# Sparse-attention layer: compressed scores that stay in PSUM, one reciprocal for two score slots at a longer pipeline distance, and query tiles assembled by DMA

## The chip, the cores and the metric

The kernel runs on one core of a Trainium2 chip. The metric is the device time of one execution in microseconds (us). The core has TensorE (PE; its weight loads are listed apart as PEld), VectorE (DVE), ScalarE (ACT), GpSimd (POOL) and SyncE (SP, which issues most of the DMAs here). L1058 means line 1058 of the kernel before, unless the text says that it is a line of the changed one.

## The reference

One layer of a decoder on x of 1 x 512 x 1024 in float32. After a norm and one input projection, two mixers run side by side: a pooling mixer, and attention with 16 heads of 64 (two groups of keys and values) in three branches: compressed keys, selected blocks, sliding window. With 512 tokens, all blocks are picked and the window covers everything, so the last two branches are plain causal attention on keys of their own. A squared-ReLU MLP follows.

```python
proj = rms_norm(x, norm_mix) @ w_in          # u, q, 3 x (k, v), gates
q  = apply_rope(q);  ks = apply_rope(ks);  kw = apply_rope(kw)
k_cmp = apply_rope(compress(kc)); v_cmp = compress(vc)     # 31 keys
p_c = masked_softmax(q @ k_cmp.T * scale);   o_c = p_c @ v_cmp
p_s = masked_softmax(q @ ks.T * scale);      o_s = p_s @ vs
p_w = masked_softmax(q @ kw.T * scale);      o_w = p_w @ vw
y_nsa = g0 * o_c + g1 * o_s + g2 * o_w
merged = g_a * (pool_mixer(u) @ w_proj_pool) + g_b * (y_nsa @ w_proj_nsa)
x = x + merged @ w_out
x = x + square(relu(rms_norm(x) @ w_ff1)) @ w_ff2
return rms_norm(x, norm_final)
```

## The kernel before

Products are made accurate by splitting each float32 operand into a high part, as float32r, and a low part, the difference; PE then multiplies high by high, high by low and low by high. A high part is a copy on ACT, a low part a subtraction on DVE (sometimes POOL).

There are three stages. The first (until about 170 us) holds the input projections and their preparation. The second is the attention stage (about 182 to 391 us), where the change lies. The third holds the output projections and the MLP.

**Slots.** The attention stage works on 8 pairs of heads with 12 slots each. A slot is one head's block of 128 queries: for the first two query blocks a slot holds both causal branches (two softmax blocks each), for the other two each branch has a slot of its own. So 96 slots hold 128 softmax blocks, and two neighbours are the two heads of a pair on the same queries. Each slot passes through this chain:

- PE computes the scores into a PSUM bank of tag S (`score_pe`, L1013, with Q against high and low keys);
- DVE adds the mask and takes the minimum in one operation (`smax`, L1035), which writes P to SBUF and the minimum into `sm`; scores are kept with their sign turned, so the minimum is the softmax's maximum;
- ACT takes the exponential with the row sum (`expo`, L1045);
- DVE inverts the sum (L1055) and POOL multiplies P by it and by the branch's gate (`weight`, L1058);
- PE transposes P into a bank of tag T (`turn_pe`, L1075), ACT copies the high part (L1086), DVE subtracts the low part (`turn_lo`, L1090);
- PE multiplies by the values into psO (`pv`, L1109). ACT and DVE empty psO (`o_evac`, L1116, L1118).

The loop over slots does the parts of several slots at each turn: scores of i+1, transposes of i − LAG, softmax of i, weights of i − 1, and PV of i − LAG − 2; with LAG 4 and five P buffers. Between them it places matmuls of the remaining projections (L394), which fill PE, and one step of each side generator. The order written here is then rearranged by a scheduler that fixes one list for each engine. PSUM has three banks of tag S, two of T, two of F (projections) and one of O.

**Side generators.** `cmp_scores(p)` handles the compressed keys of one pair, from slot 3 of the pair before: eight matmuls into psC, a bank of tag S (L950); DVE adds the mask (L957), adds the second half of the scores (L958), takes the minimum (L960) and subtracts it (L962), all but the two additions within SBUF tile `cw`; ACT takes the exponential (L965); DVE sums and inverts (L967, L968, L970); POOL weights and splits (L972, L974, L975).

`rope` prepares one pair's queries from a projection's PSUM result: ACT copies them into `rx` (L618), four DMAs on SP write the swapped halves into `rs` (L621), POOL multiplies both by cosine and sine in the attention stage (L626, L629, two of 128x256 each), DVE adds (L634, twice). Then `q_done` makes the tile Q (three buffers): ACT copies the high parts of the two heads (L659, L660) and DVE subtracts the low parts (L662, L664), each 64 partitions by 512; Q holds high and low parts of one head below each other, so that one matmul sums over both. Tiles rx and rs have one buffer each. Three of the eight pairs' queries are prepared in the first stage, five in the attention stage.

SP's queue also carries the weight loads (`raw`, L235) and parts of sums of MLP weights (L265); POOL issues other parts of these sums (L273), and does the low parts of some projection weights (L353).

Of the kernel before, what the change touches and what calls it, by code (L numbers as in the profile page):

```python
# [13 lines left out]
F32 = mybir.dt.float32  # L14
FR = mybir.dt.float32r
AF = mybir.ActivationFunctionType
# [8 lines left out]
DH = 64  # L25
NT = S // 128
S_BANKS, T_BANKS, F_BANKS = 3, 2, 2
LAG, PLAG = 4, 2
P_BUFS, PT_BUFS = 5, 3
CMP_AT = 3  # L30
BIG = 1e30
EPS = 1e-6
# [30 lines left out]
def trunk(ctx: ExitStack, tc: tile.TileContext, A, out):  # L63
# [548 lines left out]
    def rope(ps, scale, done, after=0):  # L612

        assert not scored["rope"]
        scored["rope"] = 1
        xr = ap.tile([128, S], F32, tag="rx", bufs=1, name="rx")
        sw = ap.tile([128, S], F32, tag="rs", bufs=1, name="rs")
        ACT.activation(xr, ps, AF.Copy, scale=scale)  # L618
        for b in range(4):
            a = b ^ 1  # L620
            nc.sync.dma_start(sw[32 * b:32 * b + 32, :], xr[32 * a:32 * a + 32, :])  # L621
        yield
        eng = POOL if mode["pool"] else DVE
        hs = [slice(0, S // 2), slice(S // 2, S)]
        for c in hs:
            eng.tensor_tensor(xr[:, c], xr[:, c], cosT[:, c], op=ALU.mult)  # L626
            yield
        for c in hs:
            eng.tensor_tensor(sw[:, c], sw[:, c], sinT[:, c], op=ALU.mult)  # L629
            yield  # L630
        yield
        for c in hs:
            yield
            DVE.tensor_tensor(xr[:, c], xr[:, c], sw[:, c], op=ALU.add)  # L634
        while scored["pairs"] < after:
            yield
        for _ in done(xr):
            yield
        scored["rope"] = 0

    def k_done(br):
        def done(k):
            for g in range(2):
                r = [slice(64 * h, 64 * h + 64) for h in range(2)]
                src = k[r[g], :].rearrange("p (a b) -> p a b", a=4)
                for h in range(2):
                    ACT.activation(KH[g][r[h], :, br, :], src, AF.Copy)
                yield
                DVE.tensor_tensor(KL[g][r[g], :, br, :], src, KH[g][r[g], :, br, :].bitcast(F32), op=ALU.subtract)
                yield  # L650
                ACT.activation(KL[g][r[1 - g], :, br, :], KL[g][r[g], :, br, :].bitcast(F32), AF.Copy)
        return done
# [1 line left out]
    Q = {}  # L654

    def q_done(p):
        def done(q):
            t = ap.tile([128, 2, S], FR, tag="Q", bufs=3, name="Q")
            ACT.activation(t[0:64, 0, :], q[0:64, :], AF.Copy)  # L659
            ACT.activation(t[64:128, 1, :], q[64:128, :], AF.Copy)  # L660
            yield
            DVE.tensor_tensor(t[64:128, 0, :], q[0:64, :], t[0:64, 0, :].bitcast(F32), op=ALU.subtract)  # L662
            yield
            DVE.tensor_tensor(t[0:64, 1, :], q[64:128, :], t[64:128, 1, :].bitcast(F32), op=ALU.subtract)  # L664
            Q[p] = t
        return done

# [222 lines left out]
    with ExitStack() as c2:  # L890
# [54 lines left out]
        def cmp_scores(p):  # L945
            g = p // 4
            ps = ps2.tile([128, NT, 2, 64], F32, tag="S", bufs=S_BANKS, name="psC")
            for qb in range(NT):
                for h in range(2):
                    PE.matmul(ps[:, qb, h, :], Q[p][:, h, 128 * qb:128 * qb + 128], KC[g], start=True, stop=True,  # L950
                              skip_group_check=True)
            w = p2.tile([128, NT, 2, 64], F32, tag="cw", bufs=1, name="cw")
            s8 = p2.tile([128, 3, 8], F32, tag="c8", bufs=1, name="c8")
            cm = cst[:, C_CM:C_CM + 128].rearrange("p (q n) -> p q n", q=NT)
            wl = w[:, :, :, 0:32]
            wf = w.rearrange("p q h n -> p (q h) n")[:, :, 0:32]
            DVE.tensor_tensor(wl, ps[:, :, :, 0:32], cm[:, :, None, :].to_broadcast([128, NT, 2, 32]), op=ALU.add)  # L957
            DVE.tensor_tensor(wl, ps[:, :, :, 32:64], wl, op=ALU.add)  # L958
            yield
            DVE.tensor_reduce(s8[:, 0, :], wf, axis=AX.X, op=ALU.min)  # L960
            yield
            DVE.tensor_tensor(wf, wf, s8[:, 0, :, None].to_broadcast([128, 8, 32]), op=ALU.subtract)  # L962
# [12 lines left out]
            POOL.tensor_tensor(pL, wl, pH.bitcast(F32), op=ALU.subtract)  # L975
            yield
            yield
            yield
            yield
            pt = ps2.tile([128, S], F32, tag="T", bufs=T_BANKS, name="psT")  # L980
            for qb in range(NT):
                src = PC[:, qb, :, :].rearrange("p e c -> p (e c)")
                PE.transpose(pt[:, 128 * qb:128 * qb + 128].bitcast(FR), src, identR)
            t = p2.tile([128, S], FR, tag="pc", bufs=1, name="pc")
            ACT.activation(t, pt, AF.Copy)
            PTc[p] = t
# [9 lines left out]
                        slots.append((p, 1, br, qb, h))  # L996

        live = {}
        PT = {}
        O = {}  # L1000

# [14 lines left out]
        def blocks(i):  # L1016
            p, half, br, qb, h = slots[i]
            nb = qb + 1
            if half == 0:
                return [(b, 128 * nb * b, nb) for b in range(2)]  # L1020
            return [(br, 0, nb)]

        def smax(i):
            p, half, br, qb, h = slots[i]
            ps = live[i]
            sm = p2.tile([128, 3, 2], F32, tag="sm", bufs=6, name="sm")
            P = p2.tile([128, S], F32, tag="P", bufs=P_BUFS, name="P")
            for e, (b, o, nb) in enumerate(blocks(i)):
                n = 128 * nb
# [10 lines left out]
        def expo(i):  # L1040
            p, half, br, qb, h = slots[i]
            ps, sm, P = live[i]
            for e, (b, o, nb) in enumerate(blocks(i)):
                c = P[:, o:o + 128 * nb]
                last_exp[:] = [ACT.activation(c, c, AF.Exp, bias=sm[:, 0, e:e + 1], scale=-1.0,  # L1045
                                              accum_out=sm[:, 1, e:e + 1])]

        def weight(i):
            p, half, br, qb, h = slots[i]
            ps, sm, P = live[i]  # L1050
            head = 2 * p + h
            bl = blocks(i)
            nb_ = len(bl)
            c = 3 * head + 1 + bl[0][0]
            DVE.reciprocal(sm[:, 2, 0:nb_], sm[:, 1, 0:nb_])  # L1055
            for e, (b, o, nb) in enumerate(bl):
                n = 128 * nb
                r = POOL.tensor_scalar(P[:, o:o + n], P[:, o:o + n], sm[:, 2, e:e + 1],  # L1058
# [73 lines left out]
        for i in range(n + LAG + PLAG):  # L1132
# [15 lines left out]
            if i < n:  # L1148
                smax(i)
                expo(i)  # L1150
            if 0 <= i - 1 < n:
                last = weight(i - 1)
            if i % 4 == 3 and len(begun) > 1:
                add_sum(last)
            if 0 <= t < n:
# [496 lines left out]
```

## Time and profile before

| | us |
|---|---|
| median of 3 runs | 816.5 (815.71 to 817.32) |
| profiled execution | 814.65 |
| its span, first to last instruction | 812.9 |
| PE busy | 788.6 |
| DVE busy | 627.4 |
| ACT busy | 491.6 |
| POOL busy | 207.8 |
| mean granted clock of TensorE | 0.994 |

The profile comes from the one profiled execution. "Busy" is the sum of the times in which an engine worked on at least one instruction. In a timeline a row is: start, duration, engine, line, operation, output<-inputs, shapes, count, and in brackets the idle time ahead of it with the instruction that ended it. In a group of the lines view the columns are: count, busy us, mean ns of one, idle us of the engine just before them and what ended most of it. A view by source line gives the minimum, median and maximum of one instruction's duration in ns, and the first and last start in us. In a windows view each row is a stretch, its length, busy us (and instructions) of each engine, the granted clock, and the DMA engines' share and rate.

### The profile page before, as it was taken

The page shows a single profiled execution, that of the slowest core. Times are in us where ns is not written, and L with a number is a line of the kernel's source. Part 1 is how long each engine was busy: PE and PEld are TensorE (multiplying, and loading weights), DVE is VectorE, ACT ScalarE, POOL GpSimd, SP SyncE. Part 2 cuts the span into 40 slices and gives each one's busy share as a digit, 9 for nine tenths or more (in the row PEclk, how much of TensorE's full clock was granted, in tenths as well). Part 3 has the DMA queues.
Part 4 walks back from the last instruction along what each step waited for, and adds up shares of the span by engine and source line. Part 5 has one row for each costly group of instructions (what it writes and reads, how often), then busy time and mean ns, then how long its engine had stood idle before and what let it go on. Part 6 is the DMA issues. An engine that isn't in the chain of part 4 may idle for free.

```text
span 812.9 us, 14154 instructions
## 1 busy us (share of the span) xinstructions
PE 788.6 (97%) x5163; PEld 710.2 (87%) x5163; DVE 627.4 (77%) x1217; ACT 491.6 (60%) x968; POOL 207.8 (26%) x273
## 2 busy tenths in 40 slices
PE   8999999998899999999999999999999999999996
PEld 7889878886788888888788899999999999999996
DVE  5796744539879898889664579996889688978975
ACT  6576533337777888899434466943773477347833
POOL 4000000028766867665334100111111110000000
PEclk9999999999999999999999999999999999999999
DMA  9554633357446634553964707999998997754522
GB/s 304 143 158 122 164 92 94 102 170 153 67 124 122 144 79 92 104 131 65 328 152 154 202 9 208 311 243 283 250 286 218 285 266 194 222 164 156 181 79 104
DMA packets 128752, 136.65 MB, mean 168 GB/s; under 512 B 5349, under 2 KB 117001, under 8 KB 128522
## 3 DMA queue, kind: packets, MB, share of 16 engines
q1 hardware_dynamic: 107274, 113.98, 43.5%
q0 software_dynamic: 21120, 20.97, 18.1%
q8 instruction: 41, 0.67, 0.3%
q10 hardware_dynamic: 288, 0.79, 0.3%
q14 instruction: 29, 0.24, 0.1%
HBM read 131.01 MB, written 44.04 MB: 215 GB/s over the span
## 4 chain that ended last, share of the span: by engine, by line
PE 73%; DVE 16%; ACT 6%; issue 3%; DMA 1%; POOL 1%; ACTq 0%; DVEq 0%; POOLq 0%
PE psF L394 22%; PE psB L1379 15%; PE psB L394 12%; PE psB L1498 9%; PE psO L1109 3%; PE psT L1075 3%; PE psS L1013 2%; DVE wl L308 2%; PE psV L394 2%; DVE P L1035 2%; DVE PT L1090 1%; PE psF L451 1%; ACT P L1045 1%; DVE w3l L308 1%; PE psC L714 1%
## 5 line engine op out<-in xcount | busy, mean ns | idle before, releaser
L394 PE MATMUL psF<-R,wh 128*128 128x512 f32 x512 | 166.8, 404 | 0.9 <-ACT GB L688 0.6
L306 ACT ACTIVATE wh<-raw 128x1024 fp32r<-128x1024 f32 x70 | 74.0, 1057 | 74.5 <-PE psB L1498 32.6
L351 ACT ACTIVATE wh<-raw 128x512 fp32r<-128x512 f32 (+1 forms) x100 | 60.2, 620 | 82.2 <-PE psF L394 37.4
L394 PEld LDWEIGHTS psF<-R,wh 128*128 128x128 f32 x512 | 92.5, 189 | 18.7 <-ACT GB L688 0.8
L273 POOL DMA_DIRECT2D S<-w_ff x40 | 46.3, 1158 | 233.0 <-DMA S<-w_ff 162.5
L394 PE MATMUL psF<-R,wl 128*128 128x512 f32 x256 | 101.9, 398 | 0.8 <-DVE wl L353 0.8
L1058 POOL TENSOR_SCALAR P<-P,sm,GT 128x128 f32<-128x128 f32 (+3 forms) x128 | 85.7, 702 | 47.9 <-DVE sm L1055 34.1
L308 DVE TENSOR_TENSOR wl<-raw,wh 128x1024 fp32r<-128x1024 f32 x70 | 85.3, 1220 | 16.0 <-ACT wh L306 15.9
L353 DVE TENSOR_TENSOR wl<-raw,wh 128x512 fp32r<-128x512 f32 (+1 forms) x74 | 53.5, 734 | 32.9 <-ACT wh L351 32.5
L1045 ACT ACTIVATE P<-P,sm 128x128 f32<-128x128 f32 (+3 forms) x128 | 71.1, 557 | 12.1 <-DVE sm L1035 10.8
L1035 DVE CUSTOM_DVE_ANT_0 P<-psS,cst 128x128 f32<-128x128 f32 (+3 forms) x128 | 59.6, 483 | 6.2 <-PE psT L1075 4.6
L1379 PE MATMUL psB<-R,wh 128*128 128x256 f32 x352 | 64.1, 282 | 0.0
L353 POOL TENSOR_TENSOR wl<-raw,wh 128x512 fp32r<-128x512 f32 x28 | 39.0, 1398 | 87.6 <-ACT wh L351 85.2
L306 ACT ACTIVATE w3h<-raw 128x1024 fp32r<-128x1024 f32 x35 | 37.0, 1057 | 39.0 <-PE psB L1498 16.5
L1090 DVE TENSOR_TENSOR PT<-psT,PT 128x512 fp32r<-128x512 f32 (+2 forms) x96 | 56.6, 594 | 4.6 <-ACT PT L1086 3.5
L1086 ACT ACTIVATE PT<-psT 128x512 fp32r<-128x512 f32 (+2 forms) x96 | 49.3, 521 | 15.8 <-PE psT L1075 15.1
L394 PEld LDWEIGHTS psF<-R,wl 128*128 128x128 f32 x256 | 48.3, 188 | 11.8 <-DVE wl L353 0.9
L1075 PE MATMUL psT<-ident,P 128*128 128x128 f32 x320 | 51.6, 276 | 6.4 <-POOL P L1058 5.0
L1075 PEld LDWEIGHTS psT<-ident,P 128*128 128x128 f32 x320 | 40.2, 142 | 17.0 <-POOL P L1058 7.8
L308 DVE TENSOR_TENSOR w3l<-raw,w3h 128x1024 fp32r<-128x1024 f32 x35 | 42.7, 1221 | 15.2 <-ACT w3h L306 15.2
L1379 PEld LDWEIGHTS psB<-R,wh 128*128 128x128 f32 x352 | 54.1, 189 | 0.3 <-DVE R L1321 0.2
L1379 PE MATMUL psB<-R,wl 128*128 128x256 f32 x176 | 49.5, 281 | 0.0
(385 smaller groups left out, 2303.6 us busy)
## 6 DMA issues: line engine op xcount, KB each, us to landing
raw<-w_ff SPq DMA_DIRECT2D x55, 512.0 KB, 5.0
S<-w_ff POOLq DMA_DIRECT2D x40, 512.0 KB, 7.5
raw<-S SPq DMA_DIRECT2D x40, 512.0 KB, 5.1
raw<-w_in SPq DMA_DIRECT2D x32, 512.0 KB, 4.0
S<-w_ff SPq DMA_DIRECT2D x30, 512.0 KB, 5.6
S<-S SPq DMA_DIRECT2D x10, 512.0 KB, 6.6
raw<-w_proj_nsa SPq DMA_DIRECT2D x8, 512.0 KB, 4.1
raw<-w_out SPq DMA_DIRECT2D x8, 512.0 KB, 4.4
```

Of the source, the lines that this page charges most:

```text
L306: ACT.activation(h, t, AF.Copy)
L308: DVE.tensor_tensor(l, t, h.bitcast(F32), op=ALU.subtract)
L351: ACT.activation(h[:, sl], t[:, sl], AF.Copy)
L353: eng.tensor_tensor(l[:, sl], t[:, sl], h[:, sl].bitcast(F32), op=ALU.subtract)
L394: PE.matmul(ps, a, b, start=first and j == 0, stop=last and j == n - 1, skip_group_check=True)
L1035: DVE.tensor_tensor_reduce(out=P[:, o:o + n].rearrange("p (a c) -> p a c", c=128), in0=s, in1=m, scale=1.0, scalar=3e38, op0=ALU.add, op1= ...
L1045: last_exp[:] = [ACT.activation(c, c, AF.Exp, bias=sm[:, 0, e:e + 1], scale=-1.0, accum_out=sm[:, 1, e:e + 1])]
L1058: r = POOL.tensor_scalar(P[:, o:o + n], P[:, o:o + n], sm[:, 2, e:e + 1], GT[:, qb, c + e:c + e + 1], op0=ALU.mult, op1=ALU.mult)
L1075: PE.transpose(pt[:, 128 * j:128 * j + 128], P[:, 128 * j:128 * j + 128], ident)
L1090: DVE.tensor_tensor(dL, src, dH.bitcast(F32), op=ALU.subtract)
L1379: PE.matmul(out, w[u][:, k, 128 * f:128 * f + 128], XB[x][v][:, k, :], **kw)
L1498: PE.matmul(out, YB[y][u][:, k, 128 * f:128 * f + 128], w[v][:, k, :], **kw)
```

## The change

Three parts, all in the attention stage's code; the third also touches the three query pairs that the first stage prepares.

1. In `cmp_scores` the second addition writes its sum back into psC. The minimum and the subtraction then read from psC; the subtraction still writes to `cw` in SBUF.
2. The `sm` tiles of two neighbouring slots become one (four buffers of twice the width), and `invert` takes the reciprocal of both slots' sums at once, at the odd slot (line 1059 of the changed kernel). Weights are made for slot i − 2 instead of i − 1, LAG goes from 4 to 5 and P has six buffers.
3. In `q_done` ACT copies the high part of both heads in one operation into rs, DVE subtracts the low part of both in one operation in place in rx, and four DMAs on SP place the four quarters of 64 x 512 into Q.

```diff
-LAG, PLAG = 4, 2
-P_BUFS, PT_BUFS = 5, 3
+LAG, PLAG = 5, 2
+P_BUFS, PT_BUFS = 6, 3
...
-        def done(q):
+        def done(q, other):
             t = ap.tile([128, 2, S], FR, tag="Q", bufs=3, name="Q")
-            ACT.activation(t[0:64, 0, :], q[0:64, :], AF.Copy)
-            ACT.activation(t[64:128, 1, :], q[64:128, :], AF.Copy)
-            yield
-            DVE.tensor_tensor(t[64:128, 0, :], q[0:64, :], t[0:64, 0, :].bitcast(F32), op=ALU.subtract)
-            yield
-            DVE.tensor_tensor(t[0:64, 1, :], q[64:128, :], t[64:128, 1, :].bitcast(F32), op=ALU.subtract)
+            hi, lo = other.bitcast(FR), q.bitcast(FR)
+            ACT.activation(hi, q, AF.Copy)
+            yield
+            DVE.tensor_tensor(lo, q, other, op=ALU.subtract)
+            yield
+            for h in range(2):
+                r, c = slice(64 * h, 64 * h + 64), slice(64 - 64 * h, 128 - 64 * h)
+                nc.sync.dma_start(t[r, h, :].bitcast(F32), other[r, :])
+                nc.sync.dma_start(t[c, h, :].bitcast(F32), q[r, :])
...
             DVE.tensor_tensor(wl, ps[:, :, :, 0:32], cm[:, :, None, :].to_broadcast([128, NT, 2, 32]), op=ALU.add)
-            DVE.tensor_tensor(wl, ps[:, :, :, 32:64], wl, op=ALU.add)
-            yield
-            DVE.tensor_reduce(s8[:, 0, :], wf, axis=AX.X, op=ALU.min)
-            yield
-            DVE.tensor_tensor(wf, wf, s8[:, 0, :, None].to_broadcast([128, 8, 32]), op=ALU.subtract)
+            sc = ps.rearrange("p q h n -> p (q h) n")[:, :, 0:32]
+            DVE.tensor_tensor(ps[:, :, :, 0:32], ps[:, :, :, 32:64], wl, op=ALU.add)
+            yield
+            DVE.tensor_reduce(s8[:, 0, :], sc, axis=AX.X, op=ALU.min)
+            DVE.tensor_tensor(wf, sc, s8[:, 0, :, None].to_broadcast([128, 8, 32]), op=ALU.subtract)
+            yield
...
-            sm = p2.tile([128, 3, 2], F32, tag="sm", bufs=6, name="sm")
+            if h == 0:
+                shared[0] = p2.tile([128, 3, 4], F32, tag="sm", bufs=4, name="sm")
+            b0 = h * len(blocks(i))
+            sm = shared[0][:, :, b0:b0 + len(blocks(i))]
...
+        def invert(i):
+            n = 2 * len(blocks(i))
+            DVE.reciprocal(shared[0][:, 2, 0:n], shared[0][:, 1, 0:n])
+
         def weight(i):
...
-            DVE.reciprocal(sm[:, 2, 0:nb_], sm[:, 1, 0:nb_])
...
-            if 0 <= i - 1 < n:
-                last = weight(i - 1)
+            if i < n and i % 2:
+                invert(i)
+            if 0 <= i - 2 < n:
+                last = weight(i - 2)
```

More of the change, by code (lines that the diff above doesn't have):

```diff
@@ L636, in rope @@
             yield
-        for _ in done(xr):
+        for _ in done(xr, sw):
             yield
@@ L641, in k_done, with done @@
     def k_done(br):
-        def done(k):
+        def done(k, _):
             for g in range(2):
@@ L998, in trunk @@
         live = {}
+        shared = [None]
         PT = {}
@@ L1052, in weight @@
             bl = blocks(i)
-            nb_ = len(bl)
             c = 3 * head + 1 + bl[0][0]
-            DVE.reciprocal(sm[:, 2, 0:nb_], sm[:, 1, 0:nb_])
             for e, (b, o, nb) in enumerate(bl):
```

## The prediction

> **What bounds the kernel now.** I read the page's first part, then the windows by stretch, then the waits of PE, then the timelines of the engines around each hole of PE.
>
> ```profile
> PE 788.6 (97%) x5163; PEld 710.2 (87%) x5163; DVE 627.4 (77%) x1217; ACT 491.6 (60%) x968; POOL 207.8 (26%) x273
> ```
>
> PE is the bound: 788.6 of 812.9 us. The change leaves PE's work as it is (both programs have 5155 matmuls by my count of their instructions, and the same lists from the end of the attention stage on). So it can only win where PE stands still or at a low clock, inside the attention stage.
>
> ```profile
> core 0: us, PE busy (x) PEld busy (x) DVE busy (x) ACT busy (x) POOL busy (x), PEclk, DMA share, GB/s
> 190.00:200.00 10.00, 6.87 (x33) 5.09 (x32) 9.43 (x22) 4.28 (x12) 8.09 (x12) 0.83 0.63 114
> 200.00:215.00 15.00, 14.37 (x102) 12.85 (x100) 13.73 (x50) 14.37 (x41) 10.78 (x17) 1.00 0.57 86
> 215.00:225.00 10.00, 7.44 (x38) 6.28 (x37) 8.61 (x21) 4.91 (x13) 6.67 (x10) 0.83 0.32 51
> 225.00:240.00 15.00, 14.24 (x79) 11.86 (x78) 11.72 (x36) 11.50 (x31) 9.49 (x15) 1.00 0.31 92
> 240.00:380.00 140.00, 137.93 (x895) 121.04 (x895) 124.41 (x411) 118.91 (x320) 97.93 (x134) 1.00 0.51 109
> ```
>
> From 240 to 380 us PE idles 140 − 137.93 = 2.07 us in all, while DVE is idle for 15.6. There a faster DVE buys next to nothing. Two stretches of 10 us hold idle time and a granted clock of 0.83. What PE waited for there:
>
> ```profile
> 192.98 0.44 PE L1075 MATMUL psT<-ident,P 128*128 128x128 f32 x2 [2.16 <-POOL P L1058]
> 193.76 0.44 PE L1075 MATMUL psT<-ident,P 128*128 128x128 f32 x2 [0.34 <-POOL P L1058]
> 195.75 0.87 PE L1075 MATMUL psT<-ident,P 128*128 128x128 f32 x3 [0.62 <-DVE PT L1090]
> 197.07 0.63 PE L1013 MATMUL psS<-KH,Q 128*128 128x512 f32 x1
> 197.50 0.63 PE L1013 MATMUL psS<-KL,Q 128*128 128x512 f32 x1
> 205.22 0.39 PE L1013 MATMUL psS<-KH,Q 128*128 128x512 f32 x1
> 205.45 0.39 PE L1013 MATMUL psS<-KL,Q 128*128 128x512 f32 x1
> 207.03 0.54 PE L983 MATMUL psT<-identR,PC 128*128 128x128 f32 x4 [0.63 <-DVE PT L1090]
> 217.72 0.96 PE L1075 MATMUL psT<-ident,P 128*128 128x128 f32 x4 [2.47 <-POOL P L1058]
> ```
>
> After each long hole the clock is halved for some 5 us: two score matmuls start 0.43 us apart at 197 us and 0.23 apart at 205. So a hole costs itself and about as much again. **First hole**: from 190.82 (192.98 − 2.16) until the spacing is normal again at 198.35, 7.5 us pass, in which PE does work that takes 2.4 to 2.5 at full clock: 5.0 lost (2.16 + 0.34 + 0.62 idle, about 1.9 to clock). **Second hole**: from 215.25 to the first normal spacing at 222.4, 7.2 us for 2.7 of work: 4.5 lost. With 0.63 at 207.03 and 0.76 of idle in 225 to 240, the stage loses 10.9 us before 240 and 2.1 after it.
>
> The Trainium skill's page "TensorE: Matmul & The Clock Gate", Part 1, has the clock fall to half after an idle window of about 3.4 us; by that rule holes of 2.2 and 2.5 us would cost only themselves. The trace does not agree: the two 10 us stretches around them stand at 0.83.
>
> What makes the two holes is seen on DVE and POOL:
>
> ```profile
> 189.22 4.16 DVE L962 TENSOR_TENSOR cw<-cw,c 128x256 f32<-128x256 f32 x1
> 193.31 0.68 DVE L1035 CUSTOM_DVE_ANT_0 P<-psS,cst 128x512 f32<-128x512 f32 x1
> 189.23 1.83 POOL L626 TENSOR_TENSOR rx<-rx,cst 128x256 f32<-128x256 f32 x2
> 190.63 1.78 POOL L629 TENSOR_TENSOR rs<-rs,cst 128x256 f32<-128x256 f32 x2
> 192.02 2.31 POOL L1058 TENSOR_SCALAR P<-P,sm,GT 128x256 f32<-128x256 f32 x3
> 214.47 2.79 DVE L962 TENSOR_TENSOR cw<-cw,c 128x256 f32<-128x256 f32 x1
> 214.34 1.88 POOL L626 TENSOR_TENSOR rx<-rx,cst 128x256 f32<-128x256 f32 x2
> ```
>
> The subtraction of the compressed scores, 0.41 us long when alone, lasts 4.16 and 2.79 us while POOL multiplies the rotary parts, and holds up everything queued on DVE behind it; POOL's rope stands ahead of the weights (L1058) that PE wants.
>
> **The change, part by part.** *Compressed scores kept in PSUM.* Groups of DVE in 180 to 400 us (count, busy us, mean ns, idle before):
>
> ```profile
> L962 DVE TENSOR_TENSOR cw<-cw,c 128x256 f32<-128x256 f32 x7 | 9.5, 1362 | 0.0
> L958 DVE TENSOR_TENSOR cw<-psC,cw 128x256 f32<-128x256 f32 x7 | 2.9, 416 | 0.0
> L960 DVE TENSOR_REDUCE c<-cw 128x8 f32<-128x256 f32 x7 | 2.9, 410 | 0.1
> ```
>
> The second addition already reads one operand from PSUM and takes 0.416, steadily. The subtraction will do the same: 7 × (1.362 − 0.416) = 6.6 us of DVE saved. Writing the sum into PSUM and the minimum out of it have no row; bounds are 0.41 (as now) and 0.68 (L1035's 512-wide PSUM read), and I take 0.41, the row of the same size. Against it: a bank of the three score banks stays held for two operations more.
>
> The Trainium skill's page "SBUF — State Buffer", section "Who interferes with whom", says that a DVE instruction with two SBUF inputs contends with GpSimd instructions that read SBUF, and one with at most one such input does not; it also says that the loser blocks for one whole instruction. The long L962 agrees with the first part, but 4.16 us spans more than four POOL instructions, so the loser lost again and again. By one instruction's blocking the saving would be 7 × 0.75 = 5.3 at most instead of 6.6.
>
> *One reciprocal for two slots.*
>
> ```profile
> L1013 PE MATMUL psS<-KH,Q x96: 274/392/628, 182.4 to 375.6; 128*128 128x512 f32 x48, 128*128 128x384 f32 x32, 128*128 128x256 f32 x16
> L1055 DVE RECIPROCAL sm<-sm 128x1 f32<-128x1 f32 (+1 forms) x96 | 15.0, 158 | 7.7 <-ACT P L1045 7.2
> L1058 POOL TENSOR_SCALAR P<-P,sm,GT 128x128 f32<-128x128 f32 (+3 forms) x128 | 85.7, 702 | 47.9 <-DVE sm L1055 34.1 <-PE psT L1075 5.9 <-ACT P L1045 2.9
> ```
>
> Forty-eight go: 48 × 0.158 = 7.6 us of DVE. The weights of the even slot come about a slot later, some 2 us (the last score matmul starts 193 us after the first, for 96 slots). That is what the slot more of distance (LAG 5, six P buffers) pays back. New wait: DVE at each pair's reciprocal for the second exp; behind it on DVE stand the next smax and PT subtractions, for which ACT and PE wait. Bounds: 0 (other work stands in between, and in the new order each reciprocal follows a PT subtraction or longer) and 7.2 (all of today's wait stays). Either fits DVE's 15.6 idle us.
>
> *Queries.*
>
> ```profile
> L662 DVE TENSOR_TENSOR Q<-rx,Q 64x512 fp32r<-64x512 f32 x5 | 4.3, 858 | 0.2
> L664 DVE TENSOR_TENSOR Q<-rx,Q 64x512 fp32r<-64x512 f32 x5 | 4.4, 874 | 0.2
> L660 ACT ACTIVATE Q<-rx 64x512 fp32r<-64x512 f32 x5 | 3.1, 629 | 0.1
> L621 SPq DMA_DIRECT2D rs<-rx x20: 507/583/592, 183.2 to 311.1; - x20
> DMA to landing us min/median/max: 1.9/2.9/5.0
> L664 DVE TENSOR_TENSOR Q<-rx,Q x5: 687/998/1000, 207.0 to 323.2; 64x512 fp32r<-64x512 f32 x5
> L950 PE MATMUL psC<-KC,Q x64: 191/277/297, 171.4 to 340.4; 128*128 128x64 f32 x64
> ```
>
> One subtraction and one copy of 128 rows replace two of 64 each: time goes by the 512 columns, so half is saved, 4.4 us of DVE and 3.1 of ACT. Added are 4 DMAs for each of 8 queries, 128 KB each, on SP: 4 × 0.583 = 2.3 us of issue, then 2.9 to land (nearest row: 64 KB; bounds 1.9 and 5.0, or more for twice the bytes). Q as an input of PE is in no hurry: the last one's subtraction starts at 323.2, and its compressed scores are formed up to 340.4. But rx and rs, one buffer each, are held until the DMAs have read them, and ACT's copy L618 of the next query waits for that. The weight loads behind the DMAs on SP's queue have several buffers of slack; I cost them at nothing, and they cost if a load comes over 2 us late.
>
> DVE's relief is 6.6 + 7.6 + 4.4 = 18.6 us of some 190, almost all of it hidden by PE. What counts is what becomes of the holes; I walked the changed program's order of instructions, with these durations.
>
> ```profile
> 185.58 2.84 POOL L1058 TENSOR_SCALAR P<-P,sm,GT 128x128 f32<-128x128 f32 x6
> 188.34 1.26 POOL L273 DMA_DIRECT2D S<-w_ff  x1
> L626 POOL TENSOR_TENSOR rx<-rx,cst x10: 732/745/1208, 189.2 to 316.0; 128x256 f32<-128x256 f32 x10
> ```
>
> *First hole.* In the new order PE runs on past the transposes and stops at the scores of slot 9, whose bank is freed by the new subtraction; this stands on DVE behind both rope additions L634, and these behind POOL's rope. POOL from 185.6: four 128-wide weights instead of six (4 × 0.47), a DMA issue (1.2), then rope from about 188.6, 4 × 0.745 = 191.6, for the DVE operations queued beside it read PSUM now; then the second L634 and the subtraction, 0.41 each as the others of 128x256, and two handovers of an estimated 0.1: 192.65. PE resumes there instead of at 192.98. The four 256-wide weights then run back to back, so that 0.34 and 0.62 go, but the clock is still down for 5 us. −0.3 − 0.34 − 0.62, and 0.5 back for the fuller low-clock stretch: −0.7.
>
> *The 0.63 at 207.03* stood behind a PT subtraction queued after a Q subtraction; one Q subtraction less: −0.6.
>
> *Second hole.* In the new order the weights of slots 14 to 17 come before POOL's rope, and only those of slot 18 behind it. From the end of slot 17's scores, P of slot 18 takes some 2.6 us to the reciprocal of 16 and 17 (softmax start and end on DVE and ACT), two weights (1.6 and 0.9 for the third: the mean over all widths is 0.70, and these are wide ones) and, between them, the rope (3.0): 8.1. PE has until then 22 transposes, 25 PV matmuls, 12 scores and 7 projection matmuls queued; at 0.085 for a transpose and 0.23 for each 512 columns that is 9.0. So the hole goes, with 0.9 to spare; if DVE comes 2 us late, 1.1 us of wait is left, too short to have cost the clock in before (0.63 at 207.03 did not). −4.5, of which I take −3.5.
>
> *New waits.* Two ropes follow directly on another query (pairs 4 and 5). From the end of the subtraction to the last landing: 3 × 0.58 + 2.9 = 4.6 us, with 3.2 to 4.1 of other work in between: ACT waits 0.5 to 1.4 each, of which I let 0.5 each reach PE: +1.0. Elsewhere 0.
>
> Sum: −0.7 − 0.6 − 3.5 + 1.0 = −3.8 against the profiled run's 814.65 (span 812.9 and 1.75 around it). That run lies 1.85 under the median of 816.5; on the median I predict 812.7.
>
> **Rivals.** *The hole only moves* (0.18, no change): slot 18's weights still stand behind rope, and if DVE is over 3 us late there, PE waits over 2 us again and pays for the clock. For it: 0.9 us of slack is little on a DVE that is 0.9 busy. Against: DVE loses 18.6 us of work. Time: 816.5 − 0.7 − 0.6 + 1.0 = 816.2, within 814.9 to 818.1. A measurement of this kernel can tell about 0.2%, 1.6 us, from no change.
>
> *The query DMAs block ACT* (0.28, slower): L618 waits for rx; behind it on ACT stand the exps and the PT copies, PE's transposes run out. At the median landing the wait is 0.5 to 1.4 us; from landings of about 5 us on (3 × 0.58 + 5 − 3.5 = 3.2) the hole in PE is over 2 us long, which costs the clock too, 4.5 us as the second hole did. Two places: +9 on −4.8 = +4.2, 820.7; one place, with the second hole kept: +4.5 − 1.3 = +3.2, 819.7. For it: rs landings reach 5.0 with the queues at 0.5 to 0.6 of DMA share and the new ones carry twice the bytes. Against: the median is 2.9, and ACT has 21 us idle in 240 to 380.
>
> *More holes go* (0.12): if POOL's rope no longer stretches and the subtraction gets in ahead of L634 as the engines drift, the first hole falls under the length that costs the clock too (−1.3 − 1.9 = −3.2 in place of −0.7), and the 0.76 of 225 to 240 goes: −3.8 − 2.5 − 0.8 = −7.1, with the new waits hidden as well −8.1, 808.4.
>
> *The change does not do what it says* only in one part: the Q subtraction still reads two SBUF tiles and can still be stretched (1.0 instead of 0.69 us); that is inside the sum.
>
> **How the numbers follow.** The forecast has 0.42; its own range is −6.2 (all of the second hole, the new waits hidden, and a little) to −1.7 (810.3 to 814.8). Faster by over 0.2%: 0.42 + 0.12 = 0.54; same 0.18; slower 0.28. The range must reach into both neighbours: 807.5, the larger gain and a little, to 820, between the two prices of blocked copies; this leaves out under 0.2.
>
> **What would show it.** Right: L965 (the new subtraction) at 0.41 to 0.45 in all eight; 48 reciprocals; no wait over 1 us of PE around 215 to 219, granted clock 1.0 there; PE's first hole at about 190.5 to 192.7, now on the bank (released by DVE's subtraction) and not on POOL. Wrong: ACT idle before L618 or a PE wait over 2 us near 250 to 300; PE waiting for P in the last slots; the second hole with another address; the last score matmul (375.6 before) not some 4 us earlier, or the time behind it of another length.

## The result and the profile after

The changed kernel is slower: 817.91 us median (815.81 to 821.44, 22 runs) against 815.44 (812.98 to 817.32, 22 runs), a ratio of 1.0035 with an interval of 1.0024 to 1.0046. I had forecast 812.7 against 816.5.

The first part of the page after, and its windows by the same stretches:

```profile
PE 788.0 (97%) x5163; PEld 709.9 (87%) x5163; DVE 610.3 (75%) x1161; ACT 485.4 (60%) x960; POOL 203.3 (25%) x273
190.00:200.00 10.00, 6.57 (x33) 5.57 (x32) 7.84 (x20) 4.51 (x12) 9.09 (x14) 0.83 0.74 136
200.00:215.00 15.00, 13.80 (x97) 12.07 (x97) 12.42 (x45) 12.57 (x38) 11.11 (x16) 1.00 0.83 156
215.00:225.00 10.00, 9.27 (x65) 8.02 (x64) 9.21 (x28) 8.05 (x19) 7.62 (x12) 1.00 0.35 103
225.00:240.00 15.00, 15.00 (x87) 12.88 (x86) 8.19 (x30) 10.60 (x32) 9.31 (x14) 1.00 0.65 142
240.00:380.00 140.00, 134.38 (x863) 117.55 (x862) 117.35 (x365) 112.82 (x307) 92.41 (x135) 1.00 0.50 110
```

DVE has 17 us less work, close to the sum of the parts (18.6). The second hole of before (215 to 225, clock 0.83) is gone. PE's idle time from 190 to 240 falls from 7.1 us to 5.4. But from 240 to 380, where PE had idled 2.1 us, it now idles 5.6. What ended PE's waits, from its timeline (the idle time and its releaser in brackets):

```profile
193.77 0.44 PE L1018 MATMUL psS<-KH,Q 128*128 128x384 f32 x1 [3.43 <-DVE cw L965]
211.32 0.63 PE L1086 MATMUL psT<-ident,P 128*128 128x128 f32 x4 [1.20 <-DVE PT L1101]
220.72 0.51 PE L1018 MATMUL psS<-KH,Q 128*128 128x512 f32 x1 [0.73 <-DVE sm L1043]
243.82 0.50 PE L1018 MATMUL psS<-KH,Q 128*128 128x512 f32 x1 [0.91 <-DVE sm L1043]
281.90 0.47 PE L1111 MATMUL psO<-pc,VC 128*128 128x256 f32 x2 [1.22 <-DVE oT L1129]
319.23 0.50 PE L1018 MATMUL psS<-KH,Q 128*128 128x512 f32 x1 [1.51 <-DVE sm L1043]
367.14 0.41 PE L1086 MATMUL psT<-ident,P 128*128 128x128 f32 x2 [1.17 <-DVE sm L1059]
```

All seven end on DVE work that was late, while DVE had less to do. DVE's waits and its timeline at the first hole say why for five of them, ACT's timeline explains the one at 211, and the last row, from DVE's timeline, the one at 367:

```profile
DVE rx L634 <- POOL rs L629: 7.6, 5, 2.4
190.90 2.48 DVE L634 TENSOR_TENSOR rx<-rx,rs 128x256 f32<-128x256 f32 x2 [2.22 <-POOL rs L629]
193.31 0.41 DVE L965 TENSOR_TENSOR cw<-psC,c 128x256 f32<-128x256 f32 x1
209.61 0.60 ACT L618 ACTIVATE rx<-psF 128x512 f32<-128x512 f32 x1 [1.61 <-DMA Q<-rx]
364.82 1.57 DVE L927 TENSOR_TENSOR R<-oT,R 128x256 fp32r<-128x256 f32 x1
```

Five times, 7.6 us in all, DVE stands idle at the rope additions (L634), which wait for POOL's products. Everything behind them in its fixed list waits too: the subtraction that frees the score bank, the softmax starts, the emptying of psO. Before, DVE came to these additions late enough that the product they read was done; the view of L634 showed no idle time ahead of it. At 209.61 ACT waits 1.61 us for the DMAs that place a query out of rx; the transposed P that DVE and PE need at 211 is copied behind it. The hole at 367 has a cause of its own: a subtraction of the attention output (L927) lasts 1.57 us, where the one before it took 0.44.

### The profile page after: what moved, and what is told of

Read it like the earlier page. It is cut to its first block, busy times and chain, and to the rows that moved or that the text cites. A ratio compares the mean times of both kernels' runs of the same rounds, so it can differ in the third digit from the quotient of the medians.

```text
span 814.5 us, 14158 instructions
## 1 busy us (share of the span) xinstructions
PE 788.0 (97%) x5163; PEld 709.9 (87%) x5163; DVE 610.3 (75%) x1161; ACT 485.4 (60%) x960; POOL 203.3 (25%) x273
## 4 chain that ended last, share of the span: by engine, by line
PE 71%; DVE 13%; ACT 7%; issue 3%; DMA 2%; POOL 2%; SPq 0%; DVEq 0%; ACTq 0%; POOLq 0%
PE psF L394 21%; PE psB L1392 15%; PE psB L394 12%; PE psB L1511 9%; PE psT L1086 3%; PE psO L1120 3%; PE psS L1018 2%; DVE wl L308 2%; ACT P L1053 2%; PE psV L394 2%; PE psF L451 1%; ACT PT L1097 1%; PE psC L717 1%; DVE w3l L308 1%; DVE PT L1101 1%
## 5 line engine op out<-in xcount | busy, mean ns | idle before, releaser
L306 ACT ACTIVATE wh<-raw 128x1024 fp32r<-128x1024 f32 x70 | 74.0, 1057 | 74.2 <-PE psB L1511 33.4
L1069 POOL TENSOR_SCALAR P<-P,sm,GT 128x128 f32<-128x128 f32 (+3 forms) x128 | 79.1, 643 | 46.9 <-DVE sm L1059 33.3
L353 DVE TENSOR_TENSOR wl<-raw,wh 128x512 fp32r<-128x512 f32 (+1 forms) x74 | 51.1, 701 | 32.9 <-ACT wh L351 31.7
L306 ACT ACTIVATE w3h<-raw 128x1024 fp32r<-128x1024 f32 x35 | 37.0, 1057 | 39.1 <-PE psB L1511 17.2
```

The lines of the kernel that those rows point to most:

```text
L306: ACT.activation(h, t, AF.Copy)
L353: eng.tensor_tensor(l[:, sl], t[:, sl], h[:, sl].bitcast(F32), op=ALU.subtract)
```

## Experiments

"Later rope" below means only another order in the engines' lists: the additions L634 stand behind the latest softmax start, POOL's products behind the latest weight, and the first rope of the stage starts six turns later. The kernel before, timed again beside each group of runs, took 815.5 to 816.0 us (medians).

### The three parts alone

e1 is the kernel before with the lines of part 1 of the diff, e2 with those of part 2, e3 with those of part 3:

```diff
+            DVE.tensor_tensor(ps[:, :, :, 0:32], ps[:, :, :, 32:64], wl, op=ALU.add)      # e1
...
+                invert(i)                        # e2, with LAG 5, six P buffers, weight(i - 2)
...
+                nc.sync.dma_start(t[r, h, :].bitcast(F32), other[r, :])                   # e3
```

> The kernel before with part 1 alone (compressed scores kept in PSUM). Theory A (DVE's list stands idle at the rope additions until POOL's rope is done, with the score bank held behind them; what DVE saves becomes that wait): the subtraction falls to 0.41 us, the first hole stays at 2 to 3.5 us and now ends on the bank, one or more idle stretches of DVE appear ahead of the additions; time within -1 to +2 us of before. Theory B (the later weights of part 2 and its longer distance are what costs): -3 to -5 us, as my prediction had it for the holes. Theory C (the query DMAs of part 3 are what costs): the same -3 to -5 us.

Measured: 813.38 us, ratio 0.9971 (0.996 to 0.9981). Faster by 2.1 us, between the theories: A allowed a gain of 1 at most, B and C had 3 to 5.

> The kernel before with part 2 alone (one reciprocal for two slots, LAG 5, six P buffers). Theory A: DVE has 7.6 us less work, the holes stay near 190 and 215 us since the subtraction still is stretched there; -1 to +2 us. Theory B: +2 to +4 us against before, with PE's waits on weights or reciprocals. Theory C: no change, within 1 us.

Measured: 824.27 us, ratio 1.0102 (1.0083 to 1.0122), 8.8 us slower: the way theory B said, but far beyond its range. DVE idles 7.8 us (4 times) at the additions here too, which was theory A's sign, and PE's first hole grows to 3.89.

> The kernel before with part 3 alone (query tiles placed by DMA). Theory A: within 1.5 us of before; the 0.63 us hole at 207 is gone. Theory B: -1 to 0. Theory C: +2 to +4, with idle time of ACT ahead of the copy into rx of over 3 us in all.

Measured: 820.47 us, ratio 1.0058 (1.0046 to 1.007), 5 us slower, as theory C had it. ACT's, DVE's and PE's timelines of e3:

```profile
210.94 0.60 ACT L618 ACTIVATE rx<-psF 128x512 f32<-128x512 f32 x1 [2.90 <-DMA Q<-rx]
212.90 0.41 PE L1078 MATMUL psT<-ident,P 128*128 128x128 f32 x2 [2.41 <-DVE sm L1058]
216.00 5.16 DVE L965 TENSOR_TENSOR cw<-cw,c 128x256 f32<-128x256 f32 x1
222.06 0.77 PE L1103 MATMUL psO<-pc,VC 128*128 128x256 f32 x2 [2.88 <-DVE oT L1121]
```

One wait of 2.9 us makes a hole of 2.41. What comes after is shifted so that the subtraction of the compressed scores (still within SBUF here) meets POOL's weights, rope and a split, one behind the other, and lasts 5.16 us instead of 0.41: a second hole of 2.88.

### The additions on POOL

e4, on the changed kernel:

```diff
-            DVE.tensor_tensor(xr[:, c], xr[:, c], sw[:, c], op=ALU.add)
+            eng.tensor_tensor(xr[:, c], xr[:, c], sw[:, c], op=ALU.add)
```

> The changed kernel with the two rope additions of the attention stage moved from DVE to POOL, so that DVE's list never waits for POOL's rope. Theory A: the five holes of PE that follow DVE's idle time ahead of the additions (3.4, 0.7, 0.9, 1.2, 1.5 us, in all 7.8, and the low clock after the first, about 2) go for the most part: -5 to -9 us against the changed kernel, 809 to 813. Theories B and C: within 1.5 us of the changed kernel, the holes come back elsewhere, on POOL's weights, which have 1.5 us more of work ahead of them for each query.

Measured: 828.57 us, ratio 1.0165 (1.0139 to 1.0192), 10.7 us slower than the changed kernel. The time rose against all three theories, and the wait did not go: it moved to the next instruction that reads rx, ACT's copy into rs (from ACT's waits: idle, times, longest), with the exponentials queued behind it.

```profile
ACT rs L660 <- POOL rx L634: 9.9, 4, 3.9
```

So taking the additions off DVE does not help: what costs is that a consumer of the rope stands in an engine's list ahead of work that PE needs. POOL's rope is also longer here, by two additions of about 0.73 us for each query, and how much that adds was not separated.

### A second buffer, the distance, and a later place

e5 is e3 with one line changed; e6 the kernel before with the distance alone; e7 the changed kernel with the additions bound behind the latest softmax start; e8 is e1 with the later rope.

```diff
-        xr = ap.tile([128, S], F32, tag="rx", bufs=1, name="rx")
+        xr = ap.tile([128, S], F32, tag="rx", bufs=2, name="rx")        # e5
...
-LAG, PLAG = 4, 2
-P_BUFS, PT_BUFS = 5, 3
+LAG, PLAG = 5, 2                                                        # e6
+P_BUFS, PT_BUFS = 6, 3
...
-            DVE.tensor_tensor(xr[:, c], xr[:, c], sw[:, c], op=ALU.add)
+            with behind(last_dve[0]) if last_dve else nullcontext():    # e7, e8
+                DVE.tensor_tensor(xr[:, c], xr[:, c], sw[:, c], op=ALU.add)
...
+        for _ in range(0 if not mode["pool"] else 6 if ropes[0] == 1 else 0):    # e8
+            yield
...
+            with behind(last_pool[0]) if mode["pool"] and last_pool else nullcontext():
+                eng.tensor_tensor(sw[:, c], sw[:, c], sinT[:, c], op=ALU.mult)
```

> Part 3 alone (e3) with a second buffer for rx, so that the copy of the next query need not wait for the query DMAs. Part 3 alone took 820.5 against 815.5. If ACT's wait of 2.9 us for these DMAs before that copy is the cause, the holes of 2.4 us near 213 and, with the next subtraction no longer moved into POOL's rope, of 2.9 near 222 go: 814 to 817. If the DMAs cost in another way (SP's queue, the subtraction of 128 rows, the tile Q later): 819.5 to 821.

Measured: 810.3 us, ratio 0.9935 (0.9916 to 0.9954), 10.2 us under e3 and 5.2 under the kernel before. ACT's copy waits for no DMA any more. It is the one buffer for rx, held until the DMAs have read it, that made part 3 lose. A second buffer without the DMAs was not run; in the kernel before ACT shows no wait ahead of this copy.

> The kernel before with LAG 5 and six P buffers alone, a reciprocal for each slot and the weights one turn after the softmax as before. Part 2 with both took 824.3. If the longer distance itself costs (more slots in flight, a longer end of the stage): 821 to 825. If it is the shared reciprocal (weights a turn later, and in the new list DVE standing idle ahead of the rope additions): 814 to 817.5.

Measured: 824.81 us, ratio 1.0111 (1.0084 to 1.0138): the longer distance alone costs what e2 costs. The holes lie all over the stage. The two longest (3.13 and 2.55 us) stand behind the subtraction of the compressed scores, which lasts 4.09 and 3.48 us here; DVE's idle time at the additions is 3.6 us (3 times). One hole behind the additions, from DVE's and PE's timelines:

```profile
246.41 2.19 DVE L634 TENSOR_TENSOR rx<-rx,rs 128x256 f32<-128x256 f32 x1 [1.47 <-POOL rs L629]
249.35 0.41 PE L1075 MATMUL psT<-ident,P 128*128 128x128 f32 x2 [1.22 <-DVE PT L1090]
```

> The changed kernel, where the two rope additions may not stand in DVE's list ahead of the latest softmax start traced before them; this moves them by 3 to 5 slots for three of the five queries (after softmax 32, 53, 70 instead of 29, 48, 65), the first two stay. If DVE's idle stretches ahead of the additions make the holes of 0.9, 1.2 and 1.5 us (243.8, 281.9, 319.2): -2.5 to -4 us against the changed kernel, 814 to 815.5. If the holes have another cause and the wait only sits there: within 1 us of the changed kernel's 817.9.

Measured: 815.08 us, ratio 0.9997 to the kernel before (0.9986 to 1.0008); 2.8 us under the changed kernel. As expected for DVE's idle time: PE's holes at 243.8, 281.9 and 319.2 are gone, and no hole between 240 and 380 is longer than 1.15. The one near 212 has grown, behind ACT's wait for the query DMAs (PE's timeline, ACT's waits):

```profile
212.70 0.63 PE L1090 MATMUL psT<-ident,P 128*128 128x128 f32 x4 [2.52 <-DVE PT L1105]
ACT rx L619 <- DMA Q<-rx: 2.9, 1, 2.9
```

> Part 1 alone (e1, 813.4) with the rope of the stage ordered later: additions behind the latest softmax start, POOL's four products behind the latest weight, and the first query's rope six turns later. If POOL's rope ahead of the weights makes the remaining first hole (2.2 us and the low clock after it): -2 to -5 us against e1, 808.5 to 811.5. If another wait takes its place: within 1 us of e1.

Measured: 808.22 us, ratio 0.9907 (0.9892 to 0.9922), 5.2 us under e1, a little more than the first case had. PE's first hole is 0.96 us instead of 2.18, and no half clock is recorded in the stage. Which of the three moves of the later rope does how much was not separated.

### How parts and distance combine

e9 is the whole change with the old distance; e10 parts 1 and 3 with two rx buffers and the later rope; e11 the same with the shared reciprocal at LAG 4; e12 part 1 with the distance.

```diff
-LAG, PLAG = 5, 2
-P_BUFS, PT_BUFS = 6, 3
+LAG, PLAG = 4, 2        # e9, e11
+P_BUFS, PT_BUFS = 5, 3
...
-LAG, PLAG = 4, 2
-P_BUFS, PT_BUFS = 5, 3
+LAG, PLAG = 5, 2        # e12 (on e1)
+P_BUFS, PT_BUFS = 6, 3
...
+        xr = ap.tile([128, S], F32, tag="rx", bufs=2, name="rx")    # e10, e11, with the later rope
```

> The changed kernel with LAG 4 and five P buffers, as before; the shared reciprocal and the other two parts stay. The distance alone took 824.8 against 815.5. If the distance is what the change loses by: 808 to 813, clearly under before. If the shared reciprocal needs the longer distance (weights a turn later and no turn more to use them): PE waits on weights in many slots, 818 or more. If the cost of the distance lay only in the subtraction that part 1 removes: within 1.5 us of the changed kernel's 817.9.

Measured: 816.71 us, ratio 1.0013 (1.0002 to 1.0024). Only 1.2 us under the changed kernel: taking the longer distance out of the whole change brings little, as the third case had it. Its reason does not hold, though: e12, below, shows that part 1 does not remove the price of the distance. What stands in its place is the shared reciprocal at the short distance: e14, below, which differs from e9 by it alone, took 814.0, 2.7 us less.

> Parts 1 and 3 with a second buffer for rx, LAG 4, a reciprocal for each slot, and the rope ordered later as in e8 (808.2). The DMA part with two buffers gave -5.2 alone, part 1 with the later rope -7.2. If they save different holes: 803 to 806. If the same ones: 806.5 to 809.

Measured: 807.35 us, ratio 0.9898 (0.9881 to 0.9914): the lowest median here, 0.9 us under e8; the intervals of the two overlap. The savings of the two are mostly of the same holes.

> As e10, with the shared reciprocal too, at LAG 4 and five P buffers. If the shared reciprocal is free at this distance: within 1 us of e10. If the later weights cost: 2 to 6 us slower than e10, with PE waits on weights.

Measured: 812.78 us (809.54 to 818.22), ratio 0.9965 (0.9947 to 0.9983), 5.4 us slower than e10. At this place of the rope the shared reciprocal, with the later weights that come with it, costs.

> Part 1 with LAG 5 and six P buffers, a reciprocal for each slot. Against e1 (813.4), if the distance costs by itself: +7 to +10, 820 to 823. If it costs by moving the subtraction that reads two SBUF tiles into POOL's rope, which part 1 has removed: +0 to +3, 813 to 816.5.

Measured: 819.58 us, ratio 1.0047 (1.0032 to 1.0063), 6.2 us over e1, in neither range and nearer to the first. DVE's waits in e12 hold 5.6 us at the additions:

```profile
DVE rx L634 <- POOL rs L629: 5.6, 5, 2.1
```

### The distance with the later rope, and the change without each part

e13 is e12 with the later rope, the same lines as in e8. e14, e15 and e16 are the change without part 2, 3 and 1.

```diff
+            with behind(last_dve[0]) if last_dve else nullcontext():    # e13
...
-                invert(i)                                               # e14, with LAG 4, weight(i - 1)
...
-                nc.sync.dma_start(t[r, h, :].bitcast(F32), other[r, :]) # e15
...
-            DVE.tensor_tensor(ps[:, :, :, 0:32], ps[:, :, :, 32:64], wl, op=ALU.add)    # e16
```

> e12 (part 1 with LAG 5, 819.6) with the rope ordered later as in e8. If the distance costs because DVE's list comes to the rope additions before POOL is done (5.6 us of idle there in e12): 808 to 811, near e8's 808.2. If the distance costs by itself: it stays 6 us above e8, 813 to 816.

Measured: 809.51 us, ratio 0.9928 (0.9909 to 0.9948). The distance costs 1.3 us over e8 where it cost 6.2 over e1. So most of the price is the place of the rope among the slots' instructions. In e13 DVE has no idle time ahead of the additions. In the two profiled executions the first psB matmul behind the stage starts at 388.43 (e13) and 388.20 (e8): what is left of the price lies behind the stage, where e13 loses the clock at the last hole (see the end of this text).

> The change without part 2 (parts 1 and 3, LAG 4, a reciprocal for each slot). If the parts add up: 815.5 - 2.1 + 5.0 = 818.4. If part 1 removes the stretched subtraction that followed ACT's wait for the query DMAs (a hole of 2.9 us and its low clock in e3): 812 to 815.

Measured: 814.0 us, ratio 0.998 (0.9966 to 0.9993), as the second case had it.

> The change without part 3 (parts 1 and 2). If the parts add up: 815.5 - 2.1 + 8.8 = 822. If the cost of the distance is mostly DVE's idle time at the rope additions, as in the whole change: 817 to 821, near e12's 819.6.

Measured: 817.84 us, ratio 1.0024 (1.0011 to 1.0037), as the second case had it.

> The change without part 1 (parts 2 and 3). If the parts add up: 815.5 + 8.8 + 5.0 = 829. If the holes overlap: 820 to 825.

Measured: 821.09 us, ratio 1.0063 (1.0045 to 1.008), as the second case had it.

Within the change, part 1 gains 3.2 us (821.1 to 817.9), part 2 costs 3.9 (814.0 to 817.9) and part 3 nothing (817.8 to 817.9). Alone they gave −2.1, +8.8 and +5.0. The parts do not add up, for the holes they make overlap: in e14 ACT's wait makes a hole of 2.21 us at 213, but no stretched subtraction follows it.

The shared reciprocal has no fixed price either. Pairs of runs that differ by it alone (with its later weights) give 2.7 us at LAG 4 (e9 against e14), but not at LAG 5 with the rope where the change has it: there the runs with it are 0.5 and 1.7 us faster (e2 against e6, e15 against e12).

### Sharing at its own distance, and the whole change with the later rope

e17 is e13 with the shared reciprocal, e18 the whole change with the later rope, rx with one buffer.

```diff
+                invert(i)                                               # e17, e18, with weight(i - 2)
...
+            with behind(last_dve[0]) if last_dve else nullcontext():    # e17, e18, and the other lines of e8
```

> Parts 1 and 2 (LAG 5, shared reciprocal) with the rope ordered later; differs from e13 (809.5) by the shared reciprocal alone. If sharing is free at this distance: 808.5 to 810.5; if it gives what DVE saves: under 808; if the later weights still cost: 811 to 815.

Measured: 813.74 us, ratio 0.998 (0.9964 to 0.9995), 4.2 us over e13. DVE's, POOL's and PE's timelines and a window show where most of it comes from in the profiled execution, which took 815.23:

```profile
203.60 3.00 DVE L673 TENSOR_TENSOR Q<-rx,Q 64x512 fp32r<-64x512 f32 x1
202.83 1.98 POOL L1075 TENSOR_SCALAR P<-P,sm,GT 128x512 f32<-128x512 f32 x2
204.32 1.72 POOL L353 TENSOR_TENSOR wl<-raw,wh 128x512 fp32r<-128x512 f32 x1
207.76 0.52 PE L1093 MATMUL psT<-ident,P 128*128 128x128 f32 x3 [2.35 <-DVE PT L1108]
200.00:215.00 15.00, 12.55 (x69) 11.12 (x67) 12.38 (x37) 10.92 (x33) 11.17 (x16) 0.80 0.66 100
```

Another DVE operation with both inputs in SBUF, the low part of a query, meets POOL's weights and a split and lasts 3.00 us instead of 0.69; a hole of 2.35 follows, and the stretch has a clock of 0.80. That is not all of the price: five of the twelve runs have a mean clock of 0.998 and took 812.2 to 813.2, still about 3 us over e13.

> The whole change with the rope ordered later, rx with one buffer. If the places of the rope are what the change lost by: 808 to 812, 6 to 10 us under the changed kernel. If ACT's wait for the query DMAs remains: one hole of 1 to 2.5 us near 210 and 811 to 815.

Measured: 813.84 us, ratio 0.9972 (0.9961 to 0.9984), 4.1 us under the changed kernel and 2.1 under the kernel before. The rope's place accounts for more than the whole loss, though not for the 6 to 10 us expected. ACT shows no wait for the query DMAs ahead of its copy; the one long hole left, 2.21 us at 218, follows 2.1 us of DVE's idle time at the additions of the second query. Some is given back after the stage: the first psB matmul starts at 390.31, the span ends at 811.9, 421.6 us later, where it was 417.3 before and after; in the windows of e18, PE loses 2.9 us from 470 to 520, and its waits name the weights' high parts (L306).

```profile
470.00:520.00 50.00, 47.13 (x375) 46.03 (x374) 41.75 (x55) 34.09 (x53) 3.46 (x3) 0.97 0.61 174
PE psB L1402 <- ACT wh L306: 2.0, 2, 1.3
```

## Why the prediction was wrong

Forecast: −3.8 us of the profiled run; measured: +2.5 on the medians, +1.6 from span to span. The step that failed is the one that put the longer distance and the waits at other places at nothing ("Elsewhere 0"). By its steps:

**The second hole** (−3.5): right. No wait of over 0.73 between 215 and 225, clock 1.0.

**The subtraction in PSUM**: right, 410 to 425 ns in all eight; e1 gives −2.1, e16 against the change −3.2.

**The first hole** (−0.7): right place, wrong size. PE stopped at slot 9's scores and was released by the subtraction, but at 193.77, not at 192.65. I let the second addition take 0.41. The additions also read two SBUF tiles, and POOL was at the end of its rope and then at its weights beside them: 2.48 us for the two. I gave L634 the 0.41 of operations that run undisturbed, although I had explained why L962 was long. The hole's price in clock was about right: 0.83 over 10 us is half clock for 3.4 us, 1.7 lost, not for the 5 us that I had read off the matmuls' starts. Part 1 takes the contention from one operation; here the next of its kind in DVE's list met POOL instead.

**The 0.63 at 207** (−0.6): gone, but in its place is the 1.20 at 211.32, which ACT's wait for the query DMAs made.

**The new waits** (+1.0 in the sum, rival "the query DMAs block ACT"): the rival's mechanism was real: ACT waited at one of the two ropes, 1.61 us in the change and 2.90 in e3. Alone, part 3 cost 5.0 (e3), close to the rival's 4.5 for one place, and e5 shows that it is the wait for rx that costs. In the change part 3 costs nothing on balance (e15: without it the change is as slow). That the kernel came out slower, as this rival alone had it, is luck and does not bear it out: it was slower for another reason. The weight loads behind the query DMAs, which I put at nothing, do show nothing: no wait of ACT or DVE for one stands in the changed kernel's waits from 180 to 400 us.

**The distance and the shared reciprocal at nothing**: this is the step that failed most. I took DVE's 15.6 idle us as cover for any wait up to 7.2 and the relief of 18.6 as harmless, and checked the new order only at the holes of before. But an in-order list has no cover in a mean share: DVE stood idle for 7.6 us at L634, at five places, three of them after 240 us, where I had put the new waits at 0. It does not take a faster DVE for that: e6, which saves DVE nothing, has 3.6 us of it, and e12, with part 1, 5.6. The traces show what the distance moves: one or two PT subtractions fewer stand ahead of each addition in DVE's list (since 180 us 1, 15, 23, 42 and 59 in e12, against 2, 16, 24, 44 and 60 in e1), while POOL's rope stays behind about as many weights. The distance alone costs 9.3 us (e6); with part 1 it costs 6.2 (e12 against e1), of which the later rope takes away 4.9 (e13 against e8). The shared reciprocal removes 48 instructions, but gives at most 1.7 us (at LAG 5 with the rope in its place, e15); at LAG 4 it costs 2.7, and with the later rope 4.2 to 5.4 (e17, e11). What it would cost in the whole change was not run: that would be parts 1 and 3 with the distance alone.

The views that would have told were there: DVE's groups of the kernel before from 180 to 400 us, and the timelines at the third and the fifth query.

```profile
L634 DVE TENSOR_TENSOR rx<-rx,rs 128x256 f32<-128x256 f32 x10 | 6.7, 673 | 0.0
243.91 1.44 POOL L629 TENSOR_TENSOR rs<-rs,cst 128x256 f32<-128x256 f32 x2
244.89 0.73 DVE L634 TENSOR_TENSOR rx<-rx,rs 128x256 f32<-128x256 f32 x1
316.73 1.44 POOL L629 TENSOR_TENSOR rs<-rs,cst 128x256 f32<-128x256 f32 x2
317.55 0.92 DVE L634 TENSOR_TENSOR rx<-rx,rs 128x256 f32<-128x256 f32 x1
```

There is no idle time ahead of the additions, and a mean of 673 ns where 410 is normal: they ran beside POOL's work. Each reads one of POOL's two products; at these two queries the first product was done about 0.2 and 0.1 us before DVE's addition started. At the other three DVE came 2.1 to 3.8 us after the product, at the first of them because the stretched subtraction had held it up until 193.4 (without that, in e1, DVE idles there for 1.5 us). A list that gets shorter or faster ahead of such an instruction reaches the wait sooner.

What stays open: why the shared reciprocal costs with the later rope and not where the change has the rope, and how much of its price comes from the weights being later, for no run has later weights without it. In e17's profiled execution one stretched operation with its low clock is most of it. In e11's the stage, from the first score matmul to the first psB matmul, takes 5.0 us longer than in e10's, of which 1.5 is more idle time of PE and 1.7 the lost clock at 217 (a granted clock of 0.83 from 215 to 225); five holes end on POOL's weights, 3.4 us, against four and 2.8 in e10, and the rest is not explained. And why the distance and the shared reciprocal together (e2, e15) cost no more than the distance alone (e6, e12) is not explained beyond the overlap of holes.

## What to carry to other kernels

Time saved on an engine that is not the bound can become a wait at the next instruction in its list that depends on another engine, and so can work that a new order takes from ahead of it; look for the instructions that now just miss waiting, and walk the new lists through all of them, not only through today's holes. A dependent chain of side work (here rope to Q) is best given a place behind the main work that its consumers would block; bound there, parts 1 and 3 with a second buffer for the tile that the DMAs read gave 807.35 us, 1% under the kernel before. A change of a pipeline's distance is no free companion: here it moved a side chain against the slots, and alone it cost more than anything else in the change. It has to be measured alone.

## What the runs showed of the hardware

**DVE beside POOL.** Operations of DVE with both inputs in SBUF were stretched to 5.16 us (128x256, e3), 3.00 (64x512, e17) and 2.19 (128x256, e6) where 0.41 and 0.69 are normal; the subtraction and the additions of the compressed scores with an input in PSUM stayed between 0.39 and 0.43 us in the stage in every run here, also beside POOL's work (0.41 at 193.31 in the changed kernel). The stretched ones last over several POOL instructions in a row: the 5.16 of e3 goes from 216.00 to 221.16, and POOL works from 214.73 to 220.86 on weights, rope and a split. The Trainium skill's page "SBUF — State Buffer", section "Who interferes with whom", names the pair of operands; the runs agree, and add that the wait is not bounded by one instruction.

**The clock.** The same hole does not always cost it. The last hole of the stage (PE waiting for ACT's mH) is 1.90 us in the changed kernel and 1.89 in e16; the windows from 393 to 405, first of the changed kernel, then of e16:

```profile
393.00:405.00 12.00, 10.10 (x44) 7.86 (x43) 8.96 (x11) 4.73 (x8) 4.71 (x4) 1.00 1.00 293
393.00:405.00 12.00, 10.11 (x37) 7.53 (x36) 7.71 (x10) 3.99 (x7) 4.65 (x4) 0.86 0.90 246
```

Both are busy for 10.1 us, but the one does 44 matmuls and the other 37. With LAG 4 this hole is 1.67 us, and in the nine profiles with it the first 96 psB matmuls on wh behind it, from the first start to the last, take 33.2 us. In the eleven with LAG 5 it is 1.89 to 1.91 us; in five they take 33.2 us, in six 34.7 to 34.8, with e12, e13 and e16 among them. So the distance also sets this hole, and in some executions costs 1.5 us of clock by it. Nor is a long hole sure to cost it: 2.21 us at 218 in e18 left the clock at 1.00.
